# Lone transposes between projection matmuls, and FoX q and k projected token-major: a two-layer trunk on one core

## The chip, the core and the metric

One core of a Trainium2 chip runs the whole program in one launch. The metric is device time in microseconds, the median of several executions. TensorE (PE) does the matmuls and the transposes, VectorE (DVE) and ScalarE (ACT) the arithmetic around them, GpSimd (POOL) a few memsets and small DMAs, and SyncE (SP) issues the weight DMAs. PEld is the loading of stationary operands on TensorE.

## What is computed

Two layers on 256 tokens of width 2048 (float32). Layer 0 mixes tokens with an mLSTM (4 heads), layer 1 with a softmax attention that has a forget-gate bias (FoX, 16 heads of 128). Each layer has a SwiGLU feed-forward of width 5632. The reference, cut to what matters here:

```python
for layer in range(2):
    sh1, sc1, g1, sh2, sc2, g2 = split(silu(c) @ ada_w[layer] + ada_b[layer], 6)
    h = rms_norm(x, norm_mix_w[layer]) * (1 + sc1) + sh1
    y = mlstm_mixer(h, ...) if layer == 0 else fox_mixer(h, ...)
    x = x + g1 * y
    h = rms_norm(x, norm_ffn_w[layer]) * (1 + sc2) + sh2
    g, u = split(h @ w_gate_up[layer], 2)
    x = x + g2 * ((silu(g) * u) @ w_down[layer])
return rms_norm(x, final_norm_w)

def fox_mixer(h, w_in, b_f, w_out):
    q, k, v, fl = split(h @ w_in, [2048, 4096, 6144])
    cum = cumsum(log_sigmoid(fl + b_f))              # per head
    s = q @ k.T * 128 ** -0.5 + cum[:, None] - cum[None, :]
    return (softmax(causal(s)) @ v) @ w_out
```

## The kernel before

Tokens are two blocks of 128; the model width is 16 k-tiles of 128. Weights come in tiles of four k-tiles by 512 columns (1 MB, one DMA on SP's queue), five of them buffered (`rawp`). `split` turns two k-tiles at a time into a high part (`hi`, a cast on ScalarE, L263) and a low part (`lo`, a subtraction on VectorE, L264), both in the reduced float32 form that TensorE streams once; four such pairs are buffered (`splitp`). Activations are kept transposed, width on the partitions, also as high and low part (`hT`, and `act` tiles made by `new_act`).

A projection is written in one of two ways:

- `group_a` (token-major) leaves tokens on the partitions: for each k-tile and each token block, `mm_t` issues three 512-wide matmuls (L290 high x high, L291 high x `lo`, L292 low x high) with the activation as the stationary operand. 512 columns take two PSUM banks and 16 x 6 = 96 matmuls. What has to be width-major later is turned by TensorE: `nc.tensor.transpose` of a 128x128 block through the identity, into one of two auxiliary PSUM banks (`abank`), and a copy out of it.
- `group_b` (width-major) has the weights stationary: for each k-tile and each of four column blocks a 512-wide matmul with `hi` over [high | low] tokens (L273) and a 256-wide one with `lo` over the high tokens (L276). It takes four banks and needs no turning; `total` adds the halves (L355 to L359). Only q and k of FoX, eight groups, use it.

There are six main banks (`bank`) and two auxiliary ones (`abank`). The small work (the mLSTM and FoX heads, the turns) is cut into closures in a list `steps`. `tick`, called after each block of four k-tiles, runs one or two of them (`drain(n)`); `drain()` runs all that are left. A FoX head has three steps: `scores` (logits, softmax; probabilities in `W`), `flip` (`weights_t`: three transposes of `W`), `mix` (times v, into the act tile `y`). `interleave` puts the four heads' scores first, then their flips, then their mixes. A SwiGLU group leaves two flips of four transposes each (`turned`). The normalised input of the next stage is turned by `Norm.turn`, called from `rest`. A scheduler orders instructions within each engine by its own estimates of when they are ready, so the order on an engine isn't exactly that of the code; in the bridges between stages the order is that of the code.

Of the kernel before, what the change touches and what calls it, by code (L numbers as in the profile page):

```python
# [31 lines left out]
def kernel(  # L32
# [201 lines left out]
    steps = []  # L234
    later = []

# [34 lines left out]
    def mm_b(ps, hi, lo, rhs, first, last):  # L271
        def big():
            nc.tensor.matmul(ps, hi, rhs, start=first, stop=last, skip_group_check=True)  # L273

        def little():
            nc.tensor.matmul(  # L276
                ps[:, T:], lo, rhs[:, :T], start=False, stop=False, skip_group_check=True
            )

        if last:  # L280
            little()
            big()
        else:
            big()
            little()

    def mm_t(ps, hi, lo, act, t, first, last):
        a = act[:, t * P : (t + 1) * P]
        b = act[:, T + t * P : T + (t + 1) * P]
        nc.tensor.matmul(ps, a, hi, start=first, stop=False, skip_group_check=True)  # L290
        nc.tensor.matmul(ps, a, lo, start=False, stop=False, skip_group_check=True)  # L291
        nc.tensor.matmul(ps, b, hi, start=False, stop=last, skip_group_check=True)  # L292

# [3 lines left out]

    def group_b(w, nk, c0, act, evac, bgn, adv=1):
        banks = [bank() for _ in range(4)]
        for k in range(0, nk, 4):  # L300
            ws = load_w(w, k, 4, c0)
            for m in range(4):
                cols = slice(m * P, (m + 1) * P)
                for j, (hi, lo) in enumerate(ws):
                    mm_b(
                        banks[m], hi[:, cols], lo[:, cols], act(k + j), k + j == 0, k + j == nk - 1
                    )
                if k + 4 == nk:
                    evac(m, banks[m])
            tick(bgn, adv)  # L310
# [32 lines left out]
    def turned(src, i):  # L343
        ps = abank()
        for j in range(2):
            for t in range(2):
                nc.tensor.transpose(  # L347
                    ps[:, j * T + t * P : j * T + (t + 1) * P],
                    src[:, t, (2 * i + j) * P : (2 * i + j + 1) * P], ident,
                )  # L350
        return ps.rearrange("p (k t) -> p k t", t=T)

    def total(ps, out, scale=None):
        b = t256()
        nc.scalar.activation(b, ps[:, T:], AF.Copy, scale=1.0 if scale is None else scale)  # L355
        if scale is None:
            nc.vector.tensor_tensor(out, ps[:, :T], b, op=ALU.add)
        else:
            nc.vector.scalar_tensor_tensor(  # L359
                out=out, in0=ps[:, :T], scalar=scale, in1=b, op0=ALU.mult, op1=ALU.add  # L360
            )
# [98 lines left out]
    class Norm:  # L460
# [62 lines left out]
        def rest(self, t, q):  # L523
            self.turn(t, q)
            self.affine(t, q)
# [66 lines left out]
    def carry_on(w2, hb, norm, rate):  # L592
        todo = [(0, 2), (1, 2), (0, 3), (1, 3)]

        def each(k):
            if todo:
                norm.rest(*todo.pop(0))
            if todo:
                norm.scale(*todo[0])

        for k in (4, 8):
            for n, (c, banks) in enumerate(hb.items()):
                group_a(w2, c, h_act, rate, ka=k, kb=k + 4, banks=banks, each=each if n < 2 else None)

# [87 lines left out]
    def x_block(t, j):  # L692
        ps = abank()
        for i in range(4):
            nc.tensor.transpose(
                ps[:, i * P : (i + 1) * P], xT[4 * j + i][:, t * P : (t + 1) * P], ident
            )
        nc.scalar.copy(X[:, t, 512 * j : 512 * (j + 1)], ps)

    ready_sqrt(eps_t)  # L700
    x_block(0, 0)
# [10 lines left out]
    x_block(1, 0)  # L712

    def row_scale():
        nc.vector.reciprocal(r0, r0)
        dg = t256().rearrange("p (t c) -> p t c", t=2)
        nc.vector.tensor_tensor(
            dg, ident[:, None, :].to_broadcast([P, 2, P]), r0[:, :, None].to_broadcast([P, 2, P]),
            op=ALU.mult,
        )  # L720
        ps = bank()
        nc.tensor.matmul(ps[:, :T], ones, dg, start=True, stop=True)
        nc.scalar.copy(R, ps[:, :T])
        for t in range(2):
            x_block(t, 1)
# [157 lines left out]
    def act_tile(lst, k):  # L883
        return lst[k // 2][:, k % 2, :]
# [4 lines left out]
    def weights_t(W, WT):  # L889
        ps = abank()  # L890
        for i in range(3):
            cols = slice(i * P, (i + 1) * P)
            nc.tensor.transpose(ps[:, cols], W[:, cols], ident)
        nc.scalar.copy(WT, ps[:, : 3 * P])

    def mlstm_head(hd, q, k):
# [36 lines left out]
        def flip():  # L933
            weights_t(st["W"], st["WT"])
# [28 lines left out]
        def emit():  # L963
            yt = st["yt"]
            for i in range(2):
                y[2 * hd + i] = new_act()
                ps = abank()
                for j in range(2):
                    for t in range(2):
                        nc.tensor.transpose(  # L970
                            ps[:, j * T + t * P : j * T + (t + 1) * P],
                            yt[:, t, (2 * i + j) * P : (2 * i + j + 1) * P], ident,
                        )
                for j in range(2):
                    c = 4 * hd + 2 * i + j
                    dst = y[2 * hd + i][:, j, :]
                    src = ps[:, j * T : (j + 1) * T]
                    nc.scalar.activation(dst[:, :T], src, AF.Copy, scale=nw_hs[:, c : c + 1])  # L978
                    nc.vector.scalar_tensor_tensor(
                        out=dst[:, T:], in0=src, scalar=nw_hs[:, c : c + 1],  # L980
                        in1=dst[:, :T].bitcast(F32), op0=ALU.mult, op1=ALU.subtract,
                    )

# [5 lines left out]
    def keep_t(c0, bgn, scale=None, adv=1, layer_w=0):  # L989
        if layer_w == 0:  # L990
# [5 lines left out]
            def flip():  # L996
                for i in range(2):
                    nc.scalar.copy(o[:, 2 * i : 2 * i + 2, :], turned(sp, i))
# [4 lines left out]
        group_b(w, KT, c0, h_act, lambda m, ps: total(ps, o[:, m, :], scale), bgn, adv)  # L1003
# [40 lines left out]
    def ffn(layer, begun, norm, rates, nsplit=0, srate=0.0, nxt=None):  # L1044
# [21 lines left out]
        for tq in quarters:  # L1066
            norm.rest(*tq)
# [13 lines left out]
        def swiglu(gr):  # L1081
# [10 lines left out]
            def flip(i):  # L1092
                acts[first + i] = dst = new_act()
                ps = turned(sg, i)
# [3 lines left out]
                )  # L1098

            steps.extend([lambda: flip(0), lambda: flip(1)])  # L1100

        act = lambda k: act_tile(acts, k)
        for ci, ch in enumerate(chunks):
# [4 lines left out]
            drain()  # L1108
# [24 lines left out]
    y = [None] * 8  # L1133
    vals = {}

    def fox_head(hd, q, k):
# [31 lines left out]
        def flip():  # L1168
            weights_t(st["W"], st["WT"])

        def mix():
            v, WT = vals[hd // 4][:, :, hd % 4 * P : (hd % 4 + 1) * P], st["WT"]
            if hd % 2 == 0:
                y[hd // 2] = new_act()
# [7 lines left out]
            split_act(O[:, :T], act_tile(y, hd))  # L1182
# [25 lines left out]
    for i in range(4):  # L1208
# [129 lines left out]
```

## Time and profile before

| | |
|---|---|
| median of 3 executions | 2297.38 us (2296.8 to 2297.88) |
| profiled execution | 2300.83 us, its span 2299.0 us |
| granted TensorE clock, mean | 0.999 of full |
| TensorE busy | 2275.4 us (99% of the span) |
| VectorE busy | 1612.9 us (70%) |
| ScalarE busy | 1122.8 us (49%) |
| projection matmuls L290 to L292 | 3 x 2800, means 390 to 393 ns |
| FoX q and k matmuls L273, L276 | 512 and 512, means 402 and 280 ns |

The mean of a matmul includes its passage through the array, which overlaps with that of the next; the time that one adds to a stream is the distance between starts. A line in a group of the profile can be a helper's: `turned` (L347) is used by the SwiGLU flips and by the mLSTM q and k.

### The profile page before, as it was taken

The page shows a single profiled execution, that of the slowest core. Times are in us where ns is not written, and L with a number is a line of the kernel's source. Part 1 is how long each engine was busy: PE and PEld are TensorE (multiplying, and loading weights), DVE is VectorE, ACT ScalarE, POOL GpSimd, SP SyncE. Part 2 cuts the span into 40 slices and gives each one's busy share as a digit, 9 for nine tenths or more (in the row PEclk, how much of TensorE's full clock was granted, in tenths as well). Part 3 has the DMA queues.
Part 4 walks back from the last instruction along what each step waited for, and adds up shares of the span by engine and source line. Part 5 has one row for each costly group of instructions (what it writes and reads, how often), then busy time and mean ns, then how long its engine had stood idle before and what let it go on. Part 6 is the DMA issues. An engine that isn't in the chain of part 4 may idle for free.

```text
span 2299.0 us, 26543 instructions
## 1 busy us (share of the span) xinstructions
PE 2275.4 (99%) x10376; PEld 1861.0 (81%) x10376; DVE 1612.9 (70%) x1829; ACT 1122.8 (49%) x1488; POOL 15.6 (1%) x40
## 2 busy tenths in 40 slices
PE   8999999999999999999999999999999999999998
PEld 4777878888888888888878888888888888888886
DVE  5998788878887878865687777777655554544554
ACT  3778664555543344444555444455444433444443
POOL 0000000000000000000000000000000000000000
PEclk9999999999999999999999999999999999999999
DMA  9998989798989889985667878775766555555552
GB/s 348 364 368 320 355 313 362 271 345 325 331 331 336 323 337 337 342 293 188 215 243 285 300 259 288 255 275 186 250 241 222 191 191 198 189 187 195 193 196 105
DMA packets 89090, 623.92 MB, mean 271 GB/s; under 512 B 10034, under 2 KB 10482, under 8 KB 14596
## 3 DMA queue, kind: packets, MB, share of 16 engines
q1 hardware_dynamic: 87552, 617.79, 74.3%
q0 software_dynamic: 1264, 4.29, 0.5%
q8 instruction: 81, 1.33, 0.2%
q14 instruction: 45, 0.37, 0.0%
q10 hardware_dynamic: 148, 0.14, 0.0%
HBM read 620.05 MB, written 2.13 MB: 271 GB/s over the span
## 4 chain that ended last, share of the span: by engine, by line
PE 88%; DVE 6%; DMA 3%; ACT 2%; issue 1%; SPq 0%; ACTq 0%; DVEq 0%
PE mm L292 25%; PE mm L291 25%; PE mm L290 25%; PE mm L273 5%; DVE ada L195 3%; PE mm L276 2%; DVE lo L264 2%; DMA ada<-in_ada_w_dram 2%; PE aux L347 1%; ACT hi L263 1%; DMA raw<-in_w_in_dram 1%; DMA slot<-in_w_in_dram 1%; PE aux L945 0%; PE aux L485 0%; PE aux L1144 0%
## 5 line engine op out<-in xcount | busy, mean ns | idle before, releaser
L264 DVE TENSOR_TENSOR lo<-raw,hi 128x1024 fp32r<-128x1024 f32 x764 | 926.9, 1223 | 556.8 <-ACT hi L263 556.2
L263 ACT CAST hi<-raw 128x1024 fp32r<-128x1024 f32 x764 | 797.1, 1053 | 920.3 <-PE mm L292 816.9
L291 PE MATMUL mm<-lo,hT 128*128 128x512 f32 x1840 | 718.3, 390 | 5.3 <-DVE lo L264 5.3
L290 PE MATMUL mm<-hi,hT 128*128 128x512 f32 x1840 | 719.3, 393 | 0.0
L292 PE MATMUL mm<-hi,hT 128*128 128x512 f32 x1840 | 718.1, 390 | 0.0
L195 DVE SCALAR_TENSOR_TENSOR ada<-ada,cs 128x2048 f32<-128x2048 f32 x192 | 438.9, 2286 | 49.2 <-DMA ada<-in_ada_w_dram 49.2
L291 PEld LDWEIGHTS mm<-lo,hT 128*128 128x128 f32 x1840 | 345.7, 188 | 80.1 <-DVE lo L264 10.2
L292 PEld LDWEIGHTS mm<-hi,hT 128*128 128x128 f32 x1840 | 345.4, 188 | 72.7 <-issue 0.5
L290 PEld LDWEIGHTS mm<-hi,hT 128*128 128x128 f32 x1840 | 345.3, 188 | 70.9 <-ACT hi L263 0.5
L290 PE MATMUL mm<-hi,slot 128*128 128x512 f32 x960 | 375.1, 391 | 0.2 <-ACT slot L978 0.2
L291 PE MATMUL mm<-lo,slot 128*128 128x512 f32 x960 | 374.4, 390 | 0.0
L292 PE MATMUL mm<-hi,slot 128*128 128x512 f32 x960 | 374.4, 391 | 0.0
L290 PEld LDWEIGHTS mm<-hi,slot 128*128 128x128 f32 x960 | 180.3, 188 | 37.7 <-ACT slot L978 0.8
L292 PEld LDWEIGHTS mm<-hi,slot 128*128 128x128 f32 x960 | 180.2, 188 | 37.6 <-issue 0.7
L291 PEld LDWEIGHTS mm<-lo,slot 128*128 128x128 f32 x960 | 180.2, 188 | 37.0
L273 PE MATMUL mm<-hT,hi 128*128 128x512 f32 x512 | 181.7, 402 | 0.6 <-DVE slot L359 0.6
L276 PE MATMUL mm<-hT,lo 128*128 128x256 f32 x512 | 138.3, 280 | 0.0
L273 PEld LDWEIGHTS mm<-hT,hi 128*128 128x128 f32 x512 | 94.4, 188 | 20.5 <-DVE slot L359 0.9
L276 PEld LDWEIGHTS mm<-hT,lo 128*128 128x128 f32 x512 | 96.6, 189 | 3.0
L800 ACT ACTIVATE slot<-mm 128x512 f32<-128x512 f32 x78 | 45.0, 593 | 33.9 <-PE mm L292 31.1
L435 ACT ACTIVATE t<-X 128x512 f32<-128x512 f32 x32 | 20.2, 631 | 39.2 <-DVE X L430 39.2
L1085 ACT ACTIVATE slot<-mm 128x512 f32<-128x512 f32 x44 | 25.4, 598 | 15.0 <-PE mm L292 13.8
(207 smaller groups left out, 980.5 us busy)
## 6 DMA issues: line engine op xcount, KB each, us to landing
ada<-in_ada_w_dram SPq DMA_DIRECT2D x192, 1024.0 KB, 6.5
raw<-in_gate_up_dram SPq DMA_DIRECT2D x176, 1024.0 KB, 4.9
raw<-in_down_dram SPq DMA_DIRECT2D x88, 1024.0 KB, 4.9
raw<-in_fox_in_dram SPq DMA_DIRECT2D x48, 1024.0 KB, 5.0
raw<-in_w_in_dram SPq DMA_DIRECT2D x44, 1024.0 KB, 7.3
raw<-in_w_out_dram SPq DMA_DIRECT2D x16, 1024.0 KB, 5.8
raw<-in_fox_out_dram SPq DMA_DIRECT2D x16, 1024.0 KB, 4.9
slot<-in_w_in_dram SPq DMA_DIRECT2D x16, 256.0 KB, 12.1
```

The lines of the kernel that those rows point to most:

```text
L195: nc.vector.scalar_tensor_tensor(out=raw, in0=raw, scalar=1.0, in1=cs, op0=ALU.mult, op1=ALU.mult, accum_out=acc[layer][:, j : j + 1],)
L263: nc.scalar.copy(hi, raw[:, j : j + 2, :])
L264: nc.vector.tensor_tensor(lo, raw[:, j : j + 2, :], hi.bitcast(F32), op=ALU.subtract)
L273: nc.tensor.matmul(ps, hi, rhs, start=first, stop=last, skip_group_check=True)
L276: nc.tensor.matmul(ps[:, T:], lo, rhs[:, :T], start=False, stop=False, skip_group_check=True)
L290: nc.tensor.matmul(ps, a, hi, start=first, stop=False, skip_group_check=True)
L291: nc.tensor.matmul(ps, a, lo, start=False, stop=False, skip_group_check=True)
L292: nc.tensor.matmul(ps, b, hi, start=False, stop=last, skip_group_check=True)
L347: nc.tensor.transpose(ps[:, j * T + t * P : j * T + (t + 1) * P], src[:, t, (2 * i + j) * P : (2 * i + j + 1) * P], ident,)
L435: nc.scalar.activation(t512(), X[:, t, 512 * i : 512 * (i + 1)], AF.Square, accum_out=self.ss[:, t, i : i + 1],)
L800: nc.scalar.activation(SP[i][:, t, :], banks[t], func)
L1085: nc.scalar.activation(sg[:, t, :], banks[t], AF.Silu)
```

## The change

Two things. First, a step may now be a generator that yields after each transpose. A step that is due goes onto a list `active` instead of running at once, and `poke`, called at the end of each `mm_t` (that is, after every three projection matmuls), takes the first active step up to its next yield. A step without yields runs whole at one poke. `force` finishes the first active step, `drain()` all of them; `act_tile` forces steps until the tile that a projection wants is there, so the `drain()` ahead of the down projections and between FoX's groups is gone. Second, q and k of FoX are projected by `group_a`, copied to two `t512` tiles (with the scale for q), and turned by a flip that is put at the head of the steps; two steps a tick instead of one. `group_b`, `mm_b` and `total` are removed. The core of the diff:

```diff
+    def poke():
+        if active and next(active[0], None) is None:
+            active.pop(0)
+
+    def force():
+        if not active:
+            settle()
+            active.append(run(steps.pop(0)))
+        now(active.pop(0))
...
     def drain(n=None):
+        if n is None:
+            while active or steps:
+                force()
+            return
         if steps:
             settle()
-        for _ in range(len(steps) if n is None else min(n, len(steps))):
-            steps.pop(0)()
+        active.extend(run(steps.pop(0)) for _ in range(min(n, len(steps))))
...
     def mm_t(ps, hi, lo, act, t, first, last):
...
         nc.tensor.matmul(ps, b, hi, start=False, stop=last, skip_group_check=True)
+        poke()
...
     def turned(src, i):
...
                 nc.tensor.transpose(
                     ps[:, j * T + t * P : j * T + (t + 1) * P],
-                    src[:, t, (2 * i + j) * P : (2 * i + j + 1) * P], ident,
+                    src(t)[:, (2 * i + j) * P : (2 * i + j + 1) * P], ident,
                 )
+                yield True
...
         def each(k):
             if todo:
-                norm.rest(*todo.pop(0))
+                active.append(norm.rest(*todo.pop(0)))
...
         for k in (4, 8):
+            drain()
...
     def act_tile(lst, k):
+        while lst[k // 2] is None:
+            force()
         return lst[k // 2][:, k % 2, :]
...
         o = slot().rearrange("p (k t) -> p k t", t=T)
-        group_b(w, KT, c0, h_act, lambda m, ps: total(ps, o[:, m, :], scale), bgn, adv)
+        banks = group_a(w, c0, h_act, bgn, adv)
+        sp = [t512() for _ in range(2)]
+        for t in range(2):
+            nc.scalar.activation(sp[t], banks[t], AF.Copy, scale=1.0 if scale is None else scale)
+
+        def flip():
+            for i in range(2):
+                nc.scalar.copy(o[:, 2 * i : 2 * i + 2, :], (yield from turned(lambda t: sp[t], i)))
+
+        steps.insert(0, flip)
         return o
...
             for gr in ch:
                 swiglu(gr)
-            drain()
...
-        q = keep_t(512 * i, FR, P ** -0.5, layer_w=1)
-        k = keep_t(D + 512 * i, FR, layer_w=1)
-        drain()
+        q = keep_t(512 * i, FR, P ** -0.5, 2, layer_w=1)
+        k = keep_t(D + 512 * i, FR, None, 2, layer_w=1)
```

`weights_t`, `x_block`, `Norm.rest` and the mLSTM's `emit` become generators in the same way. In the changed program the three lines of `mm_t` are L297 to L299, the transposes of `turned` L341, those of `weights_t` L889 (before L893), and the `scores` matmuls L1146 (before L1144).

TensorE, a flip of a SwiGLU group of layer 0 (`slot_4450` is the product of gate and up, `mm_4625` and `mm_4626` the two banks of the next projection). Before:

```order
L292 MATMUL mm_4625<-hi_4635,hT 128x512
L290 MATMUL mm_4626<-hi_4635,hT 128x512
L291 MATMUL mm_4626<-lo_4636,hT 128x512
L292 MATMUL mm_4626<-hi_4635,hT 128x512
L347 MATMUL aux_4664<-ident,slot_4450 128x128 x4
L290 MATMUL mm_4625<-hi_4673,hT 128x512
```

TensorE, the same flip in the changed program:

```order
L299 MATMUL mm_4625<-hi_4665,hT 128x512
L341 MATMUL aux_4676<-ident,slot_4450 128x128
L297 MATMUL mm_4626<-hi_4665,hT 128x512
L298 MATMUL mm_4626<-lo_4666,hT 128x512
L299 MATMUL mm_4626<-hi_4665,hT 128x512
L341 MATMUL aux_4676<-ident,slot_4450 128x128
```

The four transposes that stood in one row are now four rows, with three projection matmuls between.

TensorE, the projection of a k of FoX (`mm_9431` and `mm_9432` are two of its four banks). Before:

```order
L276 MATMUL mm_9431<-hT,lo_9568 128x256
L273 MATMUL mm_9431<-hT,hi_9571 128x512
L276 MATMUL mm_9431<-hT,lo_9572 128x256 x2
L273 MATMUL mm_9431<-hT,hi_9571 128x512
L273 MATMUL mm_9432<-hT,hi_9567 128x512
L276 MATMUL mm_9432<-hT,lo_9568 128x256
```

TensorE, the projection of the first k of FoX in the changed program (`t_1704` and `t_1705` hold q of the group before, one tile for each token block):

```order
L297 MATMUL mm_9387<-hi_9428,hT 128x512
L298 MATMUL mm_9387<-lo_9429,hT 128x512
L299 MATMUL mm_9387<-hi_9428,hT 128x512
L341 MATMUL aux_9439<-ident,t_1704_9382 128x128
L297 MATMUL mm_9388<-hi_9428,hT 128x512
L298 MATMUL mm_9388<-lo_9429,hT 128x512
L299 MATMUL mm_9388<-hi_9428,hT 128x512
L341 MATMUL aux_9439<-ident,t_1705_9383 128x128
```

The pairs of a 512-wide and a 256-wide matmul are gone, and the turning of the q ahead stands between the rows.

TensorE, the end of FoX, in the output projection, from the last head's `scores` to the first `mix` (L1144 and L1176 before). Before, 24 projection matmuls stand between the last `scores` (`aux_11400`) and these rows:

```order
L893 MATMUL aux_11453<-ident,slot_11324 128x128 x3
L893 MATMUL aux_11458<-ident,slot_11339 128x128 x3
L290 MATMUL mm_11542<-hi_11546,slot_10127 128x512
L291 MATMUL mm_11542<-lo_11547,slot_10127 128x512
L292 MATMUL mm_11542<-hi_11546,slot_10127 128x512
L290 MATMUL mm_11543<-hi_11546,slot_10127 128x512
L893 MATMUL aux_11463<-ident,slot_11391 128x128 x3
L893 MATMUL aux_11468<-ident,slot_11406 128x128 x3
L291 MATMUL mm_11543<-lo_11547,slot_10127 128x512
L1176 MATMUL aux_11474<-slot_11324,slot_10381 128x256
```

TensorE, the same place in the changed program; five projection matmuls stand between the last `scores` and the first of these rows (`slot_11204` holds that head's probabilities):

```order
L889 MATMUL aux_11213<-ident,slot_11141 128x128 x3
L299 MATMUL mm_11303<-hi_11306,slot_9939 128x512
L297 MATMUL mm_11302<-hi_11306,slot_9939 128x512
L889 MATMUL aux_11218<-ident,slot_11159 128x128 x3
L298 MATMUL mm_11302<-lo_11307,slot_9939 128x512
L889 MATMUL aux_11223<-ident,slot_11177 128x128 x3
L889 MATMUL aux_11228<-ident,slot_11204 128x128
L299 MATMUL mm_11302<-hi_11306,slot_9939 128x512
L889 MATMUL aux_11228<-ident,slot_11204 128x128 x2
L1178 MATMUL aux_11234<-slot_11141,slot_10246 128x256
```

The flips have moved from 24 matmuls behind the last `scores` to 5.

More of the change, by code (lines that the diff above doesn't have):

```diff
@@ L234, with run, now @@
     steps = []
+    active = []
     later = []
+    def run(f):
+        g = f()
+        if g is not None:
+            yield from g
+    def now(g):
+        for _ in g:
+            pass
+    def poke():
[6 more added lines that the diff above has]
+        now(active.pop(0))
     def settle(n=0):
@@ L296, in mm_a @@
             mm_t(ps[t], hi, lo, act, t, first, last)
[L298 to L310, printed above, removed]
     late = []
@@ L523, in rest @@
         def rest(self, t, q):
-            self.turn(t, q)
+            src = self.x[t, q // 2][:, 512 * (q % 2) : 512 * (q % 2) + 512]
+            ps = abank()
+            for j in range(4):
+                cols = slice(j * P, (j + 1) * P)
+                nc.tensor.transpose(ps[:, cols], src[:, cols], ident)
+                yield True
+            self.ps[t, q] = [ps]
             self.affine(t, q)
@@ L724, in row_scale @@
         for t in range(2):
-            x_block(t, 1)
+            now(x_block(t, 1))
     w = w_in
@@ L965, in emit @@
             for i in range(2):
[L966 to L973, printed above, removed]
+                ps = yield from turned(lambda t: yt[:, t, :], i)
+                new = new_act()
                 for j in range(2):
                     c = 4 * hd + 2 * i + j
-                    dst = y[2 * hd + i][:, j, :]
-                    src = ps[:, j * T : (j + 1) * T]
+                    dst = new[:, j, :]
+                    src = ps[:, j, :]
                     nc.scalar.activation(dst[:, :T], src, AF.Copy, scale=nw_hs[:, c : c + 1])
@@ L982, in emit @@
                     )
+                y[2 * hd + i] = new
         return [scores, flip, mix, emit]
@@ L1066, in ffn @@
         for tq in quarters:
[L1067 removed]
+            now(norm.rest(*tq))
         if nsplit:
@@ L1090, in swiglu, with flip @@
             acts.extend([None, None])
-            def flip(i):
-                acts[first + i] = dst = new_act()
-                ps = turned(sg, i)
+            def flip(acts, i):
+                ps = yield from turned(lambda t: sg[:, t, :], i)
+                dst = new_act()
                 nc.scalar.copy(dst[:, :, :T], ps)
@@ L1098, in flip @@
                 )
-            steps.extend([lambda: flip(0), lambda: flip(1)])
+                acts[first + i] = dst
+            steps.extend([lambda a=acts, i=i: flip(a, i) for i in range(2)])
         act = lambda k: act_tile(acts, k)
@@ L1133 @@
     y = [None] * 8
+    half = [None] * 8
     vals = {}
```

41 lines of the change are left out of this document (12 added, 29 removed).

## Prediction

> **What bounds the kernel now.** I read the page's busy table first, then the sliced clock row, then the chain that ended last, and then the timeline of TensorE, because the first three all name the same engine.
>
> ```profile
> span 2299.0 us, 26543 instructions
> PE 2275.4 (99%) x10376; PEld 1861.0 (81%) x10376; DVE 1612.9 (70%) x1829; ACT 1122.8 (49%) x1488; POOL 15.6 (1%) x40
> PEclk9999999999999999999999999999999999999999
> PE 88%; DVE 6%; DMA 3%; ACT 2%; issue 1%; SPq 0%; ACTq 0%; DVEq 0%
> L273 PE MATMUL mm<-hT,hi 128*128 128x512 f32 x512 | 181.7, 402 | 0.6 <-DVE slot L359 0.6
> L276 PE MATMUL mm<-hT,lo 128*128 128x256 f32 x512 | 138.3, 280 | 0.0
> L347 PE MATMUL aux<-ident,slot 128*128 128x128 f32 x208 | 30.8, 273 | 0.5 <-DVE slot L1088 0.5
> 1228.00:1457.00 229.00, 228.44 (x1283) 195.85 (x1282) 172.07 (x240) 110.38 (x186) 0.00 (x0) 1.00 0.79 281
> ```
>
> TensorE is busy 99% of the span, its granted clock is at the top in every slice, and 88% of the chain lies on it. The last row (stretch, its length, then busy time and instructions of PE, PEld, VectorE, ScalarE, GpSimd, the granted clock and the DMA share) is the FoX projection stage, the only one where the form of the projection changes: there, too, TensorE is busy 228.4 of 229.0 us, VectorE 172.1, ScalarE 110.4. So the time is the sum of what TensorE must stream, plus its few waits. Everything that the change adds to TensorE is paid in full; what it takes from VectorE or ScalarE is worth nothing by itself. The mean of a matmul (402, 280, 273 ns) is no price, since matmuls overlap; a price is the distance from one start to the next. I use this ruler, the same line at two starts with eleven matmuls between:
>
> ```profile
> 1205.92 0.39 PE L292 MATMUL mm<-hi,hT 128*128 128x512 f32 x1
> 1208.64 0.39 PE L292 MATMUL mm<-hi,hT 128*128 128x512 f32 x1
> ```
>
> 12 matmuls in 2.72 us: 0.2267 us for one 512-wide projection matmul.
>
> **Part 1: transposes from fours to singles.** By the order of the two programs, the 128x128 transposes through the identity go from 452 to 516. Before, 2 stand alone and nearly all of the others in threes, fours, sixes or eights; after, 338 stand alone, each between two projection matmuls. Of the 336 that are newly alone, 272 existed before and 64 are new. What four in a row cost, at two places:
>
> ```profile
> 649.20 0.39 PE L292 MATMUL mm<-hi,hT 128*128 128x512 f32 x1
> 649.43 0.60 PE L347 MATMUL aux<-ident,slot 128*128 128x128 f32 x4
> 650.09 0.39 PE L291 MATMUL mm<-lo,hT 128*128 128x512 f32 x1
> 2146.97 0.39 PE L292 MATMUL mm<-hi,hT 128*128 128x512 f32 x1
> 2147.88 0.40 PE L291 MATMUL mm<-lo,hT 128*128 128x512 f32 x1
> ```
>
> Between the first and the last start of each place lie the four transposes and two matmuls (L292 itself and the L290 behind the four). 0.89 and 0.91 us, less 2 x 0.2267, leave 0.44 and 0.46 us: 0.109 to 0.114 us a transpose, and I take 0.112. The trace also holds lone ones:
>
> ```profile
> 351.42 0.40 PE L291 MATMUL mm<-lo,slot 128*128 128x512 f32 x1
> 351.66 0.27 PE L970 MATMUL aux<-ident,slot 128*128 128x128 f32 x1
> 352.00 0.40 PE L290 MATMUL mm<-hi,slot 128*128 128x512 f32 x1
> 1020.68 0.39 PE L292 MATMUL mm<-hi,hT 128*128 128x512 f32 x1
> 1020.90 0.27 PE L400 MATMUL aux<-ident,mods 128*16 128x128 f32 x1
> 1021.25 0.39 PE L291 MATMUL mm<-lo,hT 128*128 128x512 f32 x1
> 1020.91 0.19 PEld L290 LDWEIGHTS mm<-hi,hT 128*128 128x128 f32 x1
> 1021.02 0.19 PEld L291 LDWEIGHTS mm<-lo,hT 128*128 128x128 f32 x1
> ```
>
> The same subtraction gives 0.58 - 0.45 = 0.127 and 0.57 - 0.45 = 0.117 us. A lone transpose is not cheaper than one of four, it is 0.005 to 0.015 dearer; I take the middle, 0.122. The two weight-load rows show why. The load for the matmul behind the transpose can start only when the transpose starts (1020.91), and the load after it follows 0.11 us later (1021.02), the moment at which the matmul really got going. Standing alone, a transpose has its own load covered by the 0.2267 us ahead of it, but is itself too short to cover much more than the next one. The 272: 272 x (0.122 - 0.112) = +2.7 us, between 272 x 0.003 = +0.8 and 272 x 0.018 = +4.9.
>
> The Trainium skill, "TensorE: Matmul & The Clock Gate", section "Step-by-step: what each phase is for", says that weight loads are pulled ahead so that the next tile's weights load while the current matmul runs, and its section on LDWEIGHTS puts a load of 128 columns at 128/1.2 ns, an estimate of 107 ns. Read one way (a run of transposes is bound by loads, a lone one has its load hidden) this speaks for the change and is the first rival; read with the load of the matmul behind the transpose, it gives the 0.11 us that the rows above show.
>
> **Part 2: q and k of FoX token-major.** Eight groups (four q, four k) had 64 pairs each of a 512-wide L273 and a 256-wide L276. Two clean stretches, 50 and 14 pairs:
>
> ```profile
> 1228.13 0.39 PE L273 MATMUL mm<-hT,hi 128*128 128x512 f32 x1
> 1245.78 0.40 PE L273 MATMUL mm<-hT,hi 128*128 128x512 f32 x1
> 1287.48 0.40 PE L273 MATMUL mm<-hT,hi 128*128 128x512 f32 x1
> 1292.34 0.39 PE L273 MATMUL mm<-hT,hi 128*128 128x512 f32 x1
> ```
>
> 17.65/50 = 0.353 and 4.86/14 = 0.347 us a pair; I take 0.351. Before: 512 x 0.351 = 179.7 us. After: 8 x 96 = 768 matmuls of 0.2267 = 174.1 us. Gain 5.6 us (3.6 to 6.6 by the two ends). But the result now lies with tokens on the partitions and must be turned: 8 transposes a group, 64 in all, every one alone in the order, 64 x 0.122 = +7.8 us (7.0 to 8.1). The turning costs more than the wider matmuls save: +2.2 us net. The evacuation changes from four halves on ScalarE and four on VectorE per group to two full ones plus two copies of turned banks on ScalarE; VectorE does 32 operations less. I cost this at nothing: by the stage's row ScalarE is idle for half of the stage. If that cover fails, the waits in Part 3 grow.
>
> **Part 3: waits.** Two waits of the trace go.
>
> ```profile
> 695.38 0.39 PE L291 MATMUL mm<-lo,slot 128*128 128x512 f32 x1
> 696.25 0.44 PE L347 MATMUL aux<-ident,slot 128*128 128x128 f32 x2 [0.48 <-DVE slot L1088]
> 1253.44 0.28 PE L276 MATMUL mm<-hT,lo 128*128 128x256 f32 x1
> 1254.27 0.51 PE L273 MATMUL mm<-hT,hi 128*128 128x512 f32 x1 [0.56 <-DVE slot L359]
> ```
>
> At 695 us the transposes of the last SwiGLU group of a chunk are drained in bulk before the down projection and wait for VectorE's product: 0.87 - 0.23 = 0.64 us. After, they are spread into the down projection, whose late k-tiles alone need them. At 1254 us a FoX group wants four banks while the one before still gives back its four: 0.83 - 0.12 = 0.71 us. A token-major group takes two of the six. Together -1.4 us.
>
> Other waits come. A FoX step used to be issued at a tick, one per four k-tiles for most heads; now a waiting step is taken up after every third matmul, so three `scores` of a layer group stand 3 matmuls apart (at the second and third q groups), and two auxiliary banks serve them. How long a bank is held, and how long a pair of scores takes to become probabilities:
>
> ```profile
> 1466.72 0.38 PE L678 MATMUL aux<-u,sel 96*128 96x512 bf16 x1
> 1470.18 0.47 ACT L1159 ACTIVATE slot<-aux,den 128x256 f32<-128x256 f32 x1
> 1474.40 0.27 PE L683 MATMUL aux<-mask,identb 128*128 128x256 bf16 x1
> 1474.51 0.82 PE L1144 MATMUL aux<-slot,slot 128*128 128x128 f32 x4
> 1475.80 1.15 DVE L1154 TENSOR_REDUCE den<-aux 128x1 f32<-128x128 f32 x4
> 1478.35 0.99 DVE L1166 TENSOR_SCALAR slot<-slot,r 128x128 f32<-128x128 f32 x4
> ```
>
> A bank is held from 1466.72 to the end of the exponential at 1470.65, 3.9 us at worst. The third `scores` comes two periods after the first, 2 x (0.8 + 0.68) = 3.0 us: it waits between 0 and 0.9 us, and I take 0.4 for each of two places, +0.8. At the end of FoX the last flips now stand right behind the last `scores`: 8 projection matmuls (1.8 us) and 9 other transposes (1.0 us) before its own probabilities are turned, where 24 matmuls stood before. The chain runs from 1475.33 (end of L1144) to 1479.34, 4.0 us, with a `lo` of VectorE inside; 4.0 - 2.8 = +1.2 us, from 0 if VectorE and ScalarE are free, to about 4 if a `lo` and another long VectorE job stand in front. What is queued behind these waits is the projection itself.
>
> In the SwiGLU groups no wait is added: a flip starts a tick after its product, and its bank is free long before the next flip. The DMA queues keep the number and order of their issues, and the clock is already full.
>
> **Sum.** +2.7 - 5.6 + 7.8 - 1.4 + 0.8 + 1.2 = +5.5 us. The profiled execution took 2300.83 us (span 2299.0 and 1.8 around it), 3.45 above the median of 2297.38; it would take 2306.3, and the median I forecast is 2302.9 us (+0.24%). What a measurement of this kernel can tell from no change is about 0.2%, 4.6 us, so 2292.8 and 2302.0 are the borders.
>
> **Rivals.**
> - *A lone transpose costs only its streaming; faster.* The mask matmul above streams 256 columns in 0.11 us (1474.40 to 1474.51), so 128 would take 0.055. Then 64 x 0.055 + 272 x (0.055 - 0.112) = -12.0, and with -5.6 - 1.4 + 2.0 the change is -17.0: 2280.4 us. That side is reached from a lone price of 0.091 us down: 336 x 0.091 = 30.6, just the 272 x 0.112 = 30.5 that go, which leaves -5. Against it stand the lone transposes in the rows, 0.117 and 0.127. Chance 7%.
> - *Nothing that can be measured.* A lone price of 0.117 and no new waits: 64 x 0.117 + 272 x 0.005 - 5.6 - 1.4 = +1.9, 2299.3 us. For it: the score chains have slack wherever VectorE is free, 57 of 229 us in the stage; against it, VectorE's long jobs cluster. Chance 33%.
> - *The new waits grow.* Each close group of `scores`, flips and `mix` steps hits a busy VectorE, 1 to 2 us at each of four q groups, and the end of FoX costs 4: 2309 us. For it: the 3.9 us for which a bank was held. Against it: that was a pair with a `lo` between. Chance 14%.
> - *That the change doesn't do what it says* is excluded by the order: the singles and the missing L273 and L276 stand there.
>
> **How the numbers follow.** The forecast, 2300.5 to 2305.5 us, has 46%. Its lower part, some 10 of the 46, lies under 2302.0. Faster by over 0.2%: 7%; within: 33 + 10 = 43%; slower: 36 + 14 = 50%. The range 2297.5 to 2309 takes in the low case at 2299.3 with its play and reaches to the large waits; the far ends and the streaming case stay outside.
>
> **What would show it.** In the changed profile: no 256-wide projection matmul, 64 more transposes, and 768 more three-line matmuls in FoX at 0.227; L299 to the second matmul behind a lone transpose at 0.57 to 0.58 us (0.51 would mean the streaming rival); 0.57 or less everywhere would cut the loss by a third. TensorE's wait at 695 us gone. New waits on ScalarE and VectorE between the second q group of FoX and its end, of 2 us in sum. I am wrong if the lone price is under 0.11, or if waits in FoX exceed 5 us.

## The result, and the profile after

The changed kernel took 2310.05 us (2309.31 to 2310.65, 4 runs) beside 2297.3 us (2296.8 to 2297.88, 4 runs) for the kernel before: a ratio of 1.0055, 95% interval 1.0038 to 1.0073, or +12.75 us. The forecast was +5.5 us, 2302.9 us, and its range ended at 2309.

The page of the changed kernel, in the rows that answer to those of before (span, busy time, granted clock, engines on the chain that ended last), and the FoX projection stage (length, then busy time and instructions of PE, PEld, VectorE, ScalarE, GpSimd, granted clock, DMA share, GB/s):

```profile
span 2308.2 us, 26105 instructions
PE 2280.2 (99%) x10184; PEld 1843.9 (80%) x10184; DVE 1603.2 (69%) x1797; ACT 1131.3 (49%) x1488; POOL 15.6 (1%) x40
PEclk9999999999999999999999999999999999999999
PE 90%; DVE 5%; DMA 2%; ACT 2%; issue 1%; SPq 0%; ACTq 0%; DVEq 0%
1225.00:1480.00 255.00, 255.00 (x1200) 204.68 (x1199) 179.66 (x231) 131.15 (x203) 0.00 (x0) 1.00 0.76 280
```

On this level nothing has happened: 99% busy, the clock at the top in every slice, and FoX without a gap. The loss shows only when the two traces are laid side by side at fixed places of the program. The table does this: the length of each stage in the profiled execution less its length in the profiled execution of before, in us. It begins at the first mixing matmul of the mLSTM (L945 before, L942 after), because the profiled execution of before was some 3 us slower up to there (292.04 us, against 288.1 to 290.6 in the others, d1 apart) and 3.5 us above its median. The end of the mLSTM runs from there to the first transpose of the first bridge; the bridge to its last matmul L556 / L547; FoX from its gates to the first transpose of the third bridge. The labels are those of the experiments below.

| | end of mLSTM | first bridge | SwiGLU 0, second bridge | FoX and its output | rest | sum |
|---|---|---|---|---|---|---|
| changed kernel | +4.10 | +3.10 | +0.80 | +3.19 | +1.29 | +12.48 |
| a1_mlstm_whole | +0.06 | +0.02 | +0.61 | +3.25 | +1.55 | +5.49 |
| a2_bridge_free | +5.56 | -0.42 | +2.47 | +2.91 | +1.37 | +11.89 |
| a3_both | +0.08 | -0.44 | +1.77 | +3.56 | +1.35 | +6.32 |
| a4_groups_again | +5.50 | +4.76 | -1.15 | +1.39 | -0.08 | +10.42 |
| b1_fox_back | +4.24 | +3.19 | +1.05 | +0.22 | +1.27 | +9.97 |
| b2_fox_alone | +0.02 | +0.05 | -0.42 | +3.11 | -0.03 | +2.73 |
| b3_jobs_into_bridge | +0.03 | +2.02 | +0.58 | +2.72 | -0.05 | +5.30 |
| b4_mlstm_whole_groups | +0.06 | +0.01 | -1.13 | +0.99 | +0.17 | +0.10 |
| c1_jobs_later | +0.83 | -0.37 | +7.99 | +2.44 | +1.31 | +12.20 |
| c2_jobs_later_two | +0.13 | +1.59 | +2.87 | +4.00 | +1.32 | +9.91 |
| c3_best_guess | +0.01 | -0.01 | -1.53 | +0.53 | +0.29 | -0.71 |
| d1_jobs_retimed | -0.70 | -0.40 | +1.70 | +2.42 | +1.27 | +4.29 |

The last three stages of the changed kernel, where the prediction had its terms, cost 5.28 us. The other 7.2 us stand at two places for which it had none. TensorE's longest waits of the whole run (engine, line, awaited line; us in total, times, longest) name them; of the last two rows, 0.8 and 0.6 us lie in the later bridges:

```profile
PE aux L341 <- DVE slot L954: 3.2, 2, 3.1
PE mm L547 <- DVE hT L495: 2.6, 2, 1.8
PE aux L470 <- DVE slot L459: 1.9, 3, 1.3
```

**The end of the mLSTM.** VectorE there, first in the changed kernel, then before (start, length, operation, and in brackets the idle time ahead of it and its releaser):

```profile
334.16 2.28 DVE L195 SCALAR_TENSOR_TENSOR ada<-ada,cs 128x2048 f32<-128x2048 f32 x1
336.37 0.16 DVE L951 RECIPROCAL hrs<-hrs 128x2 f32<-128x2 f32 x1
336.45 1.20 DVE L287 TENSOR_TENSOR lo<-raw,hi 128x1024 fp32r<-128x1024 f32 x1
337.57 0.15 DVE L952 TENSOR_TENSOR hrs<-hrs,r 128x2 f32<-128x2 f32 x1
338.40 1.23 DVE L287 TENSOR_TENSOR lo<-raw,hi 128x1024 fp32r<-128x1024 f32 x1 [0.68 <-ACT hi L286]
339.54 1.41 DVE L954 SCALAR_TENSOR_TENSOR slot<-aux,hrs,slot 128x512 f32<-128x512 f32 x2
```

```profile
335.37 0.17 DVE L954 RECIPROCAL hrs<-hrs 128x2 f32<-128x2 f32 x1
335.56 0.16 DVE L955 TENSOR_TENSOR hrs<-hrs,r 128x2 f32<-128x2 f32 x1
335.76 1.41 DVE L957 SCALAR_TENSOR_TENSOR slot<-aux,hrs,slot 128x512 f32<-128x512 f32 x2
337.09 1.22 DVE L264 TENSOR_TENSOR lo<-raw,hi 128x1024 fp32r<-128x1024 f32 x1
```

`ada` (L195) is a background job: a 2.2 us piece of the modulation vectors that are wanted a stage later. Before, the third head's reciprocal and its normalisation follow each other in 0.4 us and the two `lo` wait. After, a `lo` has come between the two small operations, and a second one, which itself waits 0.68 us for ScalarE, ahead of the normalisation: 3.2 us from reciprocal to L954. A part of this order is in the code already. `tick` calls `drain` and then issues the background jobs. Before, `drain` issued the whole step, with its VectorE operations, ahead of the job and of the next `lo`; after, it only puts the step on the list, and the step's operations are issued at the pokes, behind both. The first half of that product lets TensorE go on:

```profile
336.89 0.39 PE L299 MATMUL mm<-hi,slot 128*128 128x512 f32 x1
340.34 0.48 PE L341 MATMUL aux<-ident,slot 128*128 128x128 f32 x1 [3.06 <-DVE slot L954]
341.00 1.76 PE L341 MATMUL aux<-ident,slot 128*128 128x128 f32 x7 [0.18 <-DVE slot L954]
342.46 0.80 PE L297 MATMUL mm<-hi,slot 128*128 128x512 f32 x1
340.00:344.00 4.00, 3.48 (x12) 2.75 (x13) 4.00 (x7) 1.37 (x4) 0.00 (x0) 0.57 1.01 428
```

The wait is 3.06 us, and it isn't the whole price: the seven transposes behind it take 1.46 us to the next start, 0.209 each, where a group takes 0.11, and the last row gives a granted clock of 0.57 for these 4 us. The page's clock row, in slices of 58 us, can't show that.

**The first bridge.** VectorE in the changed kernel:

```profile
425.66 0.68 DVE L414 TENSOR_TENSOR t<-mm,slot 128x512 f32<-128x512 f32 x1
426.26 2.28 DVE L195 SCALAR_TENSOR_TENSOR ada<-ada,cs 128x2048 f32<-128x2048 f32 x1
428.47 0.69 DVE L415 TENSOR_TENSOR X<-X,t 128x512 f32<-128x512 f32 x1
432.14 1.37 DVE L482 TENSOR_SCALAR t<-aux,mods 128x128 f32<-128x128 f32 x4 [1.19 <-PE aux L470]
433.43 2.29 DVE L195 SCALAR_TENSOR_TENSOR ada<-ada,cs 128x2048 f32<-128x2048 f32 x1
435.65 0.69 DVE L495 TENSOR_TENSOR hT<-t,hT 128x512 fp32r<-128x512 f32 x1
```

Two `ada` stand inside the chain residual, norm, modulation, on which TensorE waits (1.29 us for L459, then 1.79 us for L495). Before, one stood there, behind the residual's sum X, where ScalarE's part of the norm covers half of it, and none between `t` and `hT`:

```profile
425.61 0.69 DVE L430 TENSOR_TENSOR X<-X,t 128x512 f32<-128x512 f32 x1
426.22 2.29 DVE L195 SCALAR_TENSOR_TENSOR ada<-ada,cs 128x2048 f32<-128x2048 f32 x1
430.30 1.37 DVE L497 TENSOR_SCALAR t<-aux,mods 128x128 f32<-128x128 f32 x4 [1.19 <-PE aux L485]
431.77 0.69 DVE L510 TENSOR_TENSOR hT<-t,hT 128x512 fp32r<-128x512 f32 x1
```

That the order in the bridges is that of the code holds for the bridge's own operations alone. The code issues these `ada` behind the bridge (a2 and b3 below change what is issued there, and with it what stands inside), and the scheduler put them in between.

### The profile page after: what moved, and what is told of

The parts are those of the page before. It is cut to its first block, busy times and chain, and to the rows that moved or that the text cites. A ratio compares the mean times of both kernels' runs of the same rounds, so it can differ in the third digit from the quotient of the medians.

```text
span 2308.2 us, 26105 instructions
## 1 busy us (share of the span) xinstructions
PE 2280.2 (99%) x10184; PEld 1843.9 (80%) x10184; DVE 1603.2 (69%) x1797; ACT 1131.3 (49%) x1488; POOL 15.6 (1%) x40
## 3 DMA queue, kind: packets, MB, share of 16 engines
q0 software_dynamic: 1264, 4.29, 0.5%
q8 instruction: 79, 1.29, 0.2%
## 4 chain that ended last, share of the span: by engine, by line
PE 90%; DVE 5%; DMA 2%; ACT 2%; issue 1%; SPq 0%; ACTq 0%; DVEq 0%
PE mm L299 28%; PE mm L298 28%; PE mm L297 28%; DVE ada L195 2%; DVE lo L287 2%; DMA ada<-in_ada_w_dram 2%; PE aux L341 1%; ACT hi L286 1%; PE aux L942 0%; PE aux L1146 0%; PE mm L547 0%; PE mm L543 0%; PE aux L1178 0%; PE mm L544 0%; PE aux L889 0%
## 5 line engine op out<-in xcount | busy, mean ns | idle before, releaser
L297 PE MATMUL mm<-hi,hT 128*128 128x512 f32 x2096 | 843.4, 404 | 0.0
L298 PE MATMUL mm<-lo,hT 128*128 128x512 f32 x2096 | 818.1, 390 | 3.6 <-DVE lo L287 3.6
L299 PE MATMUL mm<-hi,hT 128*128 128x512 f32 x2096 | 819.2, 391 | 0.0
L297 PEld LDWEIGHTS mm<-hi,hT 128*128 128x128 f32 x2096 | 393.7, 188 | 97.0 <-ACT slot L794 0.2
L195 DVE SCALAR_TENSOR_TENSOR ada<-ada,cs 128x2048 f32<-128x2048 f32 x192 | 438.7, 2285 | 33.3 <-DMA ada<-in_ada_w_dram 32.6
L299 PEld LDWEIGHTS mm<-hi,hT 128*128 128x128 f32 x2096 | 393.4, 188 | 84.1 <-issue 0.5
L298 PEld LDWEIGHTS mm<-lo,hT 128*128 128x128 f32 x2096 | 394.8, 188 | 77.8 <-DVE lo L287 7.4
L297 PE MATMUL mm<-hi,slot 128*128 128x512 f32 x960 | 379.5, 395 | 0.0
L299 PE MATMUL mm<-hi,slot 128*128 128x512 f32 x960 | 374.5, 390 | 0.0
L297 PEld LDWEIGHTS mm<-hi,slot 128*128 128x128 f32 x960 | 180.6, 188 | 39.9 <-issue 0.5
L299 PEld LDWEIGHTS mm<-hi,slot 128*128 128x128 f32 x960 | 180.3, 188 | 37.8 <-DVE slot L970 0.4
L341 PE MATMUL aux<-ident,slot 128*128 128x128 f32 x240 | 60.3, 278 | 3.2 <-DVE slot L954 3.2
L341 PEld LDWEIGHTS aux<-ident,slot 128*128 128x128 f32 x240 | 33.4, 143 | 13.3 <-DVE slot L954 4.3
L415 DVE TENSOR_TENSOR X<-X,t 128x512 f32<-128x512 f32 x48 | 32.3, 686 | 0.5
L806 ACT COPY mm<-slot 128x512 f32<-128x512 f32 x56 | 31.4, 590 | 0.2
```

The costliest lines, as they stand in the source:

```text
L195: nc.vector.scalar_tensor_tensor(out=raw, in0=raw, scalar=1.0, in1=cs, op0=ALU.mult, op1=ALU.mult, accum_out=acc[layer][:, j : j + 1],)
L341: nc.tensor.transpose(ps[:, j * T + t * P : j * T + (t + 1) * P], src(t)[:, (2 * i + j) * P : (2 * i + j + 1) * P], ident,)
L415: nc.vector.tensor_tensor(cols, cols, m, op=ALU.add)
L806: nc.scalar.copy(banks[t], SP[i][:, t, :])
```

## The experiments

Theory 1: the arithmetic on TensorE and FoX cost about what was forecast, and some 7 us come from VectorE's order at these two places. Rival A: lone transposes are dearer than their rows show. Rival B: q and k of FoX carry the loss. Theory 2, formed later: the split mLSTM steps stall by themselves, whatever else stands on VectorE. The differences to the kernel before are ratio less one times its median, in us, with the 95% interval.

**a1_mlstm_whole.** Steps run whole at their tick until the mLSTM's output projection.

```diff
...
-        active.extend(run(steps.pop(0)) for _ in range(min(n, len(steps))))
+        for _ in range(min(n, len(steps))):
+            active.append(run(steps.pop(0)))
+            if not lone[0]:
+                now(active.pop(0))
...
+    lone[0] = True
+
     def project_out(wo, res, bgn, adv, upto, norm, w2, heads):
```

> The changed kernel, but the steps of the first layer's mLSTM are issued whole at their tick, as before the change; from the output projection of that layer on everything is as in the changed kernel. In the program's order VectorE then does the same work in the same order as before the change at two places, the end of the mLSTM and the first bridge. Theory 1 (some 5.5 us of the 12.75 are the arithmetic on TensorE and the waits of FoX, some 7 are background jobs of VectorE that the new order put in front of work that TensorE waits for, at these two places): +4.5 to +6.5 us to the kernel before, 2302 to 2304 us; by the traces the mLSTM's end costs 0 to 1 us and the bridge 0 to 1 us more than before. Rival A (a lone transpose costs more than the 0.120 us that the trace shows, wherever it stands): some 120 of the 336 new lone ones go, so a third of the loss goes, +8 us. Rival B (the whole loss lies in q and k of FoX): unchanged, +12 to +13 us.

Measured +4.6 us (2.5 to 6.4), 2303.84 us. By the orders of the two programs 322 of the 338 lone transposes stay (only 16 go, not the 120 that the expectation for rival A supposed), and both stalls are gone: +0.06 and +0.02 us. Of all TensorE waits between 290 and 450 us these are left:

```profile
PE aux L474 <- DVE slot L463: 0.2, 1, 0.2
PE aux L946 <- DVE slot L974: 0.2, 1, 0.2
PE mm L301 <- ACT slot L973: 0.2, 1, 0.2
```

Rival B falls (FoX is as in the changed kernel, +3.25), and so does A: with 95% of the lone transposes still there, the whole change costs 4.6 us. The code of the bridge and of all that follows is that of the changed kernel, so the bridge's order came down from the mLSTM's.

**a2_bridge_free.** Three background jobs are held back behind the first bridge.

```diff
         if nsplit:
+            credit[0] = -3.0
             for tq in ((1, 2), (0, 3), (1, 3)):
```

> The changed kernel, but the background jobs (`ada`) are held back by three at the start of the first SwiGLU part, so that none stands inside the first bridge; they run three ticks or so later. The end of the mLSTM is as in the changed kernel. Theory 1: the bridge gives back the 3.1 us that it lost, and perhaps 1.3 us more, since before the change one such job already stood ahead of a reciprocal there: +8.3 to +9.7 us to the kernel before. Rival A (price of lone transposes): unchanged, +12 to +13 us, since no transpose moves. Rival B (FoX): unchanged, +12 to +13 us. A later `ada` may come too late for its consumer at the end of the SwiGLU part; the trace would show TensorE waiting for it there.

Measured +11.0 us (8.3 to 13.8), above the expected range, which the interval takes in. The bridge did give back its 3.1 us and 0.4 more, with no transpose moved. The sum missed, for two reasons in the table: 1.7 us came back in the SwiGLU part (two waits of 0.6 us for `lo`), and the end of the mLSTM, with the same wait of 3.06 us, cost 1.5 us more, since the low clock lasted longer:

```profile
340.00:344.00 4.00, 3.26 (x11) 2.37 (x11) 3.64 (x5) 0.95 (x2) 0.00 (x0) 0.50 1.01 428
344.00:348.00 4.00, 4.00 (x10) 2.54 (x10) 3.06 (x6) 1.16 (x3) 0.00 (x0) 0.66 0.95 389
```

**a3_both.** Both edits.

> Both of the edits above: mLSTM steps whole at their tick, and three background jobs held back behind the first bridge. Theory 1: the two places are independent and the sum holds, +3.5 to +5.5 us to the kernel before (2301 to 2303 us): 5.5, less up to 1.3 us for the background job that stood in the bridge before the change too. Rival A: +8 us. Rival B: +12 to +13 us.

Measured +4.8 us (2.8 to 6.7). Holding jobs back is worth nothing once the order is right: 0.44 us in the bridge, given back as `lo` waits.

**a4_groups_again.** A step, once taken up, issues all its transposes.

```diff
-        if active and next(active[0], None) is None:
-            active.pop(0)
+        if active:
+            now(active.pop(0))
```

> The changed kernel, but a waiting step, once taken up between matmuls, issues all its transposes at once (in twos, threes, fours or eights) and not one at a time. q and k of FoX stay token-major. VectorE's order at the end of the mLSTM and in the first bridge stays as in the changed kernel. Theory 1: only the price of standing alone goes, 336 x (0.120 - 0.112) = 2.7 us: 1.5 to 3.5 us faster than the changed kernel, +9 to +11 us to the kernel before. Rival A (lone transposes are all of the loss): +0 to +3 us to the kernel before. Rival B: q and k keep the loss, +12 us.

Measured +8.7 us (6.0 to 11.5), 0.3 below the expectation. Behind the first bridge, 5.1 us are saved; ahead of it the same waits stand, dearer by 3.1 us. In this bridge the clock went down behind a gap of only 2.2 us from start to start:

```profile
437.50 0.39 PE L544 MATMUL mm<-slot,hT 128*128 128x512 f32 x1
439.72 1.39 PE L547 MATMUL mm<-slot,hT 128*128 128x512 f32 x4 [1.84 <-DVE hT L495]
440.91 0.63 PE L543 MATMUL mm<-slot,hT 128*128 128x512 f32 x1
441.34 0.63 PE L544 MATMUL mm<-slot,hT 128*128 128x512 f32 x1
```

0.43 us from start to start, where 0.227 is the rule, until 443.9 us. The changed kernel has the same gap without it.

**b1_fox_back.** The changed kernel, with `group_b` for q and k again, `poke` after every second pair, `drain()` behind k.

```diff
...
-        q = keep_t(512 * i, FR, P ** -0.5, 2, layer_w=1)
-        k = keep_t(D + 512 * i, FR, None, 2, layer_w=1)
+        q = keep_t(512 * i, FR, P ** -0.5, layer_w=1)
+        k = keep_t(D + 512 * i, FR, layer_w=1)
+        drain()
```

> The changed kernel, but q and k of FoX are projected feature-major again, with their 512-wide and 256-wide pairs, so that their 64 transposes go; a waiting step is still taken up between the pairs, one transpose at a time, and what waits is drained behind k, as before the change. The end of the mLSTM and the first bridge stand as in the changed kernel. Theory 1 (now with its terms from the traces: FoX +3.2, two places in the first layer +7.2, the rest of the SwiGLU parts +2): the stage of FoX falls back to its length before, within 1 us, and the whole is +9 to +10 us to the kernel before. Rival B (the loss lies in q and k of FoX): 0 to +2 us.

Measured +9.9 us (7.1 to 12.6); FoX is back to +0.22. Rival B falls a second time.

**b2_fox_alone.** The kernel before, with the token-major q and k, turned in fours (two steps of four transposes and a copy, at the head of `steps`).

> The kernel before, and of the change only this: q and k of FoX projected token-major and turned, each bank's four transposes in a row. Everything ahead of FoX is as before. Theory 1: -5.6 for the matmuls, 64 x 0.112 = +7.2 for the transposes, -0.7 for the wait at 1254 us that goes, and 0 to +2 for new waits in FoX: +1 to +3 us; no stage outside FoX moves by over 0.3 us. Rival B: +12 us.

Measured +1.6 us (-0.5 to +3.4), as expected for the whole, but the trace has a surprise: of its +3.11 in FoX and its output, 2.3 are a wait at the third bridge, where no instruction was moved. (The first SwiGLU part, too, moved by more than the 0.3 us allowed, by -0.42.) The next run shows the same.

**b3_jobs_into_bridge.** The kernel before, with one more job at the start of the SwiGLU part; nothing else.

```diff
         if nsplit:
+            bg(1.0)
             for tq in ((1, 2), (0, 3), (1, 3)):
```

> The kernel before, with one background job (`ada`) issued at the start of the first SwiGLU part, ahead of the ticks there, so that three of them stand inside the first bridge: ahead of the first reciprocal, between the residual's product and its sum, and ahead of the modulation. No transpose moves and no matmul changes. Theory 1: the bridge alone grows, by 2.5 to 4.5 us, with TensorE waiting there for VectorE, and the whole by as much. If jobs issued earlier save waits later, a part is given back. Rivals A and B: 0.

Measured +2.8 us (0.5 to 5.1). The first bridge grew by 2.02 us (waits of 1.26 and 0.70), less than the 2.5 us expected at least: the mechanism at the size of one job, in a kernel without a single new lone transpose. Of the rest of the trace's +5.3, 1.8 are again a wait at the third bridge:

```profile
1551.11 2.29 DVE L195 SCALAR_TENSOR_TENSOR ada<-ada,cs 128x2048 f32<-128x2048 f32 x1 [4.09 <-DMA ada<-in_ada_w_dram]
1553.33 0.69 DVE L429 TENSOR_TENSOR t<-mm,slot 128x512 f32<-128x512 f32 x1
1556.69 1.06 PE L485 MATMUL aux<-ident,slot 128*128 128x128 f32 x8 [1.82 <-DVE slot L474]
```

Here an `ada` stands at the head of VectorE's queue and waits 4.09 us for its DMA, and the residual, which is ready, waits behind it. The kernel before has the same order; there this `ada` started at 1549.57, 1.5 us earlier, and TensorE, which came to this place 0.4 us later, didn't wait. In b3 the DMA was issued at 1543.67 us, before at 1544.72, so it took longer; why isn't known.

**b4_mlstm_whole_groups.** a1 and a4 together.

> The changed kernel with the mLSTM's steps whole at their tick (as in the first of these experiments) and, from there on, all transposes of a waiting step issued at once. q and k of FoX are token-major. Theory 1: no lone transposes and none of the two stalls: of the changed kernel's loss stay -5.6 + 7.2 for q and k, -1.4 for the two waits that went, and 0 to +2 of waits in FoX: 0 to +2.5 us to the kernel before, and 2 to 4.5 us faster than with lone transposes. Rival B: +12 us.

Measured +1.1 us (-0.9 to +3.0). Without stalls and without lone transposes the change costs nothing that can be told; its FoX stage is +0.99, and -5.6 + 64 x 0.112 - 0.7 is +0.9.

**c1_jobs_later, c2_jobs_later_two.** All transposes stay split; 3 (or 2) background jobs are put off ahead of the last mLSTM unit.

```diff
+    credit[0] -= 3.0
     unit(7, start[7], KT, LR[3], AF.Sigmoid)
```

> The changed kernel, with the credit for background jobs of VectorE (`ada`) lowered by 3 ahead of the last mLSTM projection unit. Every step is still split into single transposes between projection matmuls, q and k of FoX are token-major; only the background jobs run later, and some transposes at the end of the mLSTM stand a few matmuls away from where they stood. In VectorE's order no `ada` stands any longer inside the first bridge, and `hrs` and the normalisation of the mLSTM's third head follow each other with no `lo` between. Theory 1 (order on VectorE is the cause, not the transposes): both stalls go, so that 5.5 to 7 of the 12 us come back: +5 to +7 us to the kernel before; up to 1.5 us may be given back where the jobs run later, as when three were held back behind the bridge alone. Theory 2 (the split mLSTM steps themselves take too long, whatever stands on VectorE): the stall of 3 to 5 us at the end of the mLSTM stays, +9 to +10 us.

> As the kernel above, with the credit lowered by 2: VectorE's order then has one `ada` straight ahead of `hrs` at the end of the mLSTM, and 25 projection matmuls (5.7 us) stand on TensorE between the third head's mixing and its transposes; in the first bridge one `ada` stands ahead of the first modulated sum. Theory 1: the mLSTM's end costs 0 to 2 us, the bridge 0 to 1.5 us: +6 to +9 us to the kernel before. Theory 2: +9 to +11 us.

c1 measured +10.3 us (7.1 to 13.6), c2 +7.4 (4.4 to 10.1). In c1 both places are free, as theory 1 has it and against theory 2, and yet the time, for which theory 1 had +5 to +7, is as bad as ever: the jobs have a due time, and three were made up in a row straight behind the bridge's chain. VectorE and TensorE there, where half the clock (granted 0.55 and 0.60 in the two stretches of 4 us from 444 us) adds to the waits:

```profile
432.01 2.29 DVE L195 SCALAR_TENSOR_TENSOR ada<-ada,cs 128x2048 f32<-128x2048 f32 x1
434.22 2.29 DVE L195 SCALAR_TENSOR_TENSOR ada<-ada,cs 128x2048 f32<-128x2048 f32 x1
436.43 2.29 DVE L195 SCALAR_TENSOR_TENSOR ada<-ada,cs 128x2048 f32<-128x2048 f32 x1
443.06 0.50 PE L297 MATMUL mm<-hi,hT 128*128 128x512 f32 x1 [2.87 <-ACT hT L505]
445.22 0.80 PE L299 MATMUL mm<-hi,hT 128*128 128x512 f32 x1 [1.20 <-DVE hT L495]
```

c2's sum was in its range by other parts than expected (mLSTM +0.13, bridge +1.59, but the part behind it +2.87).

**c3_best_guess.** b4 with `group_b` for FoX, as in b1.

> What the runs so far speak for: steps of the mLSTM whole at their tick, transposes of a step issued at once, q and k of FoX feature-major as in the kernel before, and of the change only this, that what waits at the end of a SwiGLU chunk is spread into the down projection. By the traces the first SwiGLU part gains 1.1 us with it and the second 0; no bridge gets a stall. Theory 1: -1.5 to 0 us to the kernel before, which is below what this measurement can tell. Theory 2: the same.

Measured 2296.9 us beside 2298.22, -1.8 us (-3.9 to +0.2): not told from the kernel before.

**d1_jobs_retimed.** The changed kernel, three jobs earlier, three fewer at the mLSTM's last unit, three behind the bridge.

```diff
     for i in range(4, 6):
+        credit[0] += 1.5
         unit(i, start[i], KT, LR[0], AF.Sigmoid)
...
+    credit[0] -= 3.0
     unit(7, start[7], KT, LR[3], AF.Sigmoid)
...
         if nsplit:
+            credit[0] = -3.0
```

> The changed kernel with every step still split into single transposes and q and k of FoX token-major; only the times of the background jobs of VectorE (`ada`) move: three are issued earlier, ahead of the mLSTM's last gates, three fewer during its last unit, and three are held back behind the first bridge. No job is left over to be made up in the bridge, as it was when they were only put off. In VectorE's order the normalisation of the third head follows its reciprocal with no `lo` between, and no `ada` stands in the first bridge; on TensorE some transposes at the end of the mLSTM stand a few matmuls away from where they stood. Theory 1: both stalls go, 1 to 1.5 us is given back as waits for `lo` in the SwiGLU part, as when three were held back alone: +5 to +7.5 us to the kernel before. Theory 2 (the split mLSTM steps stall by themselves): the end of the mLSTM keeps its 4 to 5.5 us, +10 to +12 us.

Measured +11.3 us (8.0 to 14.5): a miss, though the two places are free (-0.70, -0.40). Its row of the table sums to +4.29 because the table starts behind the place where it now pays: from the mLSTM's gates to its first transposes it takes 7.05 us longer than before, with jobs one after the other on VectorE, and TensorE waiting (in the first row for ScalarE, which itself had waited 2.27 us for VectorE):

```profile
226.62 1.17 PE L297 MATMUL mm<-hi,hT 128*128 128x512 f32 x2 [3.06 <-ACT hi L286]
229.34 0.79 PE L298 MATMUL mm<-lo,hT 128*128 128x512 f32 x1 [1.54 <-DVE lo L287]
```

The two waits are 4.6 us; behind them, until 233.3 us, the matmuls stand 0.43 us apart.

So it is shown that the stalls at both places are VectorE's order (they go when the jobs go, and the bridge's comes when a job is put there), and that the split steps don't stall by themselves. By the traces, none of four other timings of the jobs with split steps (a2, c1, c2, d1) got the 7 us back; each paid somewhere else. The runs alone leave it open for c2, whose interval begins at +4.4. In the first layer VectorE has little room: 313.32 of the 362 us from 60 to 422 us are busy in the kernel before (87%), against 1261.64 of 1868 us (68%) behind. Whether some timing suits the split steps is open.

## Why the prediction was wrong

- **The step that failed** is the list of new waits in Part 3. It put them in FoX and at its end, and closed the SwiGLU groups; the end of the mLSTM, whose steps are split by the same edit, and the bridges got no term at all, which is a price of nothing without a cover named. They cost 4.1 and 3.1 us. That VectorE was busy for 12.32 of the 14 us of the first bridge (422 to 436 us, before) speaks for a price of its order there. The order was compared on TensorE, where the transposes had moved, not on VectorE, where `ada` and `lo` had come to stand in other places: at the mLSTM in part because a step that waits for the pokes issues its VectorE operations behind the tick's job and the next `lo`, and in the bridge by the scheduler. How much of the first stall is the code's order, and how much the scheduler's, isn't shown. Neither sign that the prediction gave for being wrong (a lone price under 0.11, waits in FoX over 5 us) came.
- **The waits of FoX** (+0.8 and +1.2) didn't come: in the changed kernel TensorE waits nowhere in the projections and heads of FoX. (In a1 one such wait stands there, 0.6 us for ScalarE's L1167.) FoX measured +3.2; the terms that lie there (-5.6 + 7.8 - 0.7, and 0.4 for the 36 older transposes newly alone) make +1.9, with the waits +3.9. Of the 1.3 us beyond the +1.9, 0.4 are a wait at the third bridge; the rest isn't settled.
- **The price of a lone transpose.** Rows of the changed kernel in the second SwiGLU part:

```profile
1708.79 0.39 PE L299 MATMUL mm<-hi,hT 128*128 128x512 f32 x1
1709.02 0.27 PE L341 MATMUL aux<-ident,slot 128*128 128x128 f32 x1
1709.04 0.47 PE L297 MATMUL mm<-hi,hT 128*128 128x512 f32 x1
1709.36 0.39 PE L298 MATMUL mm<-lo,hT 128*128 128x512 f32 x1
```

  0.57 us less two matmuls is 0.117; averaged over about a hundred such places of this part it is 0.120, and the interval ahead is 0.0025 longer, 0.1225 in all, against 0.111 in fours. The step of 0.010 was right. The first rival, 0.055, is excluded. From a1 to b4, 319 lone transposes go: 3.4 us by the two ratios (each known to about 2), 5.4 by the single traces, where 319 x 0.011 is 3.5; what the trace has beyond that isn't settled.
- **q and k**: b4's +0.99 in FoX against +0.9 from the terms. Right. **The two waits** at 695 and 1254 us are gone. Right.
- Without the two stalls (a1) the change costs +4.6 us by the runs and +5.5 by the trace: the sum of the prediction, for a kernel that is not the one it was made for. That they agree is in part luck, since the 2.0 us of waits in that sum didn't come. The third rival had the size (2309 us) and the kind (VectorE's long jobs in front of work that TensorE waits for), but in FoX.

## What to carry to other kernels

When an edit defers work, or passes through a list scheduler, compare the order on every engine that feeds the bound one, at every place where slack is small, and not only on the engine and in the stage that the edit is about. Long background jobs on a busy engine are a price that travels: take one out of a chain and look at once where it lands, what it is due for, and whether it waits for a DMA at the head of the queue.

## What the runs showed of the hardware

A wait on TensorE can cost more than its length. After 3.06 us of it, transposes started 0.209 us apart instead of 0.11 and 512-wide matmuls 0.43 instead of 0.227, for about 3.4 us in the changed kernel and about 6 in a2, behind the same wait. The Trainium skill, "TensorE: Matmul & The Clock Gate", in "Part 1: The HAM clock gate", says that the array falls to half rate after an idle window of about 3.4 us and that the window runs free of the program. The half rate and its uneven length agree. In a4, though, half rate began behind a gap of 2.2 us between starts, with shorter waits ahead of it, and in c1 the matmuls behind a wait of 2.87 us started 0.34 and then 0.23 us apart, while half rate (0.43) began behind the next wait, of 1.20 us; so a single gap under 3.4 us is no safety.
